# Layer 0's feed-forward network in two passes, context tokens first and then latent tokens by seven block products, with layer 1's last modulation moved into mixer 1

## The chip, the cores and the metric

The kernel runs on one core of one Trainium2 chip. The metric is the device time of one execution in microseconds. A run of this kernel is repeated, and the median stands; a profiled execution has a span (first to last instruction of the trace) and a device time of its own, a little longer than the span.

In the profile PE is TensorE (matrix products), PEld its loading of stationary operands, DVE is VectorE, ACT ScalarE, POOL GpSimd, and SP the engine that issues nearly all transfers. Engines run their instructions in order, each from a queue that is fixed when the kernel is built.

## The reference, cut to what matters

Two layers work on 512 latent tokens and 256 context tokens of width 1024. Each has a mixer (attention with input and output projections) and a SwiGLU feed-forward network (FFN) with 2816 hidden units. Every part is preceded by an RMS norm with shift and scale, and followed by a gate, all three from a modulation: a product of silu(c) with a matrix of 1024 x 6144 per layer.

```python
for l in range(DEPTH):
    last = l == DEPTH - 1
    mx = (s_c @ mod_w[l] + mod_b[l])[:, None, :]
    mc = (s_cc @ mod_w[l] + mod_b[l])[:, None, :]
    shx1, scx1, gx1, shx2, scx2, gx2 = jnp.split(mx, 6, axis=-1)
    ...
    x = x + gx1 * ax
    x = x + gx2 * _swiglu(_rms(x, norm_ffn_w[l]) * (1.0 + scx2) + shx2, ffn_w_in[l], ffn_w_out[l])
    if not last:
        ctx = ctx + gc1 * ac
        ctx = ctx + gc2 * _swiglu(_rms(ctx, norm_ffn_w[l]) * (1.0 + scc2) + shc2, ffn_w_in[l], ffn_w_out[l])

def _swiglu(h, w_in, w_out):
    gate, up = jnp.split(h @ w_in, 2, axis=-1)
    return (jax.nn.silu(gate) * up) @ w_out
```

After layer 0 both streams go on; layer 1's FFN is for the latent tokens only. Parts 0 to 5 of a modulation are shift, scale and gate of the mixer, then shift, scale and gate of the FFN.

## The kernel before: how the work is staged

All fp32 products are made of three products of fp32r pieces: an operand is split into a rounded high part and the rest, and high x high, high x low and low x high are summed in PSUM. So every weight that comes in by a transfer is cast on ACT (the high part) and subtracted on DVE or POOL (the low part) before TensorE may use it.

The stages in order are: start and modulation of layer 0; mixer 0 in four head groups; out-projection; layer 0's FFN; mixer 1 with eight heads, whose projections run a head ahead of the attention; out-projection; layer 1's FFN. Tile schedules the instructions by their order in the program and by its own estimate of times; where the program pins an engine's instructions, their order in that engine's queue is the program's.

Layer 0's FFN (`ffn`, called near the end of the layer 0 part) goes over hidden units in 11 pairs of 128. For each 128 it makes the gate and the up product for 512 latent and 256 context tokens together (L814: matmuls of 512 and of 256 columns, each with its own load of weights), then the hidden units, and for each pair the down products into `dps` (L869 to L871), which are gated and added to the residual by DVE (L439, L440). The modulation of layer 1 (24 chunks of 256 columns, `mod_chunks_by_pool`) is spread over these pairs by `MODS1`: ACT scales the rows (L213), POOL adds them up (L214 to L219), and TensorE then sums over partitions and turns the result (`modrow` L224, `modcol` L232) for up to four sums at a time. Context and latent tokens meet at the end in `done0`, the norm for layer 1.

Layer 1's FFN (`ffn_by_blocks`) treats 512 latent tokens and 128 hidden units at a time. Hidden blocks 0 to 3 are plain products; from block 4 on the gate and up products are made of seven products of half-size blocks in place of eight, each of 12 matmuls of 256 columns. That needs sums of weight blocks on POOL (`combine`, the tiles `ws`), sums of activation blocks once (`terms`, the tiles `tf`), and sums of the products on DVE (`after`). All instructions of this function are pinned.

Two rooms matter below. `raw_tile` has two slots for the whole kernel; out-projection weights, the rows of `ffn_w_out` (`wdr`), and the weights of mixer 1's projections (`wir`, L327, cast at L334, subtracted by POOL at L321) all land in it, and a slot is free again when the last reader is done. The pool `wr` of `ffn_by_blocks` has four slots, two hidden blocks' worth of gate and up weights.

Of the kernel before, what the change touches and what calls it, by code (L numbers as in the profile page):

```python
# [10 lines left out]
F32 = mybir.dt.float32  # L11
# [26 lines left out]
MODS1 = (2, 2, 2, 2, 2, 3, 3, 4, 4, 0)  # L38
# [25 lines left out]
def backbone(es: ExitStack, tc: tile.TileContext, x, c, ctx, c_ctx, mod_w, mod_b, norm_mix_w, norm_ffn_w,  # L64
# [11 lines left out]
    sc_pool = tc.tile_pool(name="p_sc", bufs=2, space=PSUM, reuse_waits="tile")  # L76
# [91 lines left out]
    def mod_chunk(l, part, n, new_tile, pool, bank, wide=None, room=("modr", 1)):  # L168
# [3 lines left out]
        ps = p_1.tile([P, width], F32, name="mod", tag=bank) if wide is None else \  # L172
            wide.tile([P, 1024], F32, name="mod", tag="sc")[:, :width]
# [7 lines left out]

        for i, k in enumerate([*range(kp, KT), *range(kp)]):
# [14 lines left out]
    def mod_chunks_by_pool(chunks, pool):  # L197
# [3 lines left out]
        for l, part, n, streams in chunks:  # L201
            c0 = part * D + n * width
            accs = [pool.tile([P, width], F32, name="ma", tag="ma", bufs=4) for _ in range(streams)]
            for pc in range(2):
# [3 lines left out]
                for i, acc in reversed(list(enumerate(accs))):  # L208

                    pr = pool.tile([P, 4, width], F32, name="modp", tag="mp", bufs=1) if i else w  # L210
                    for k in range(4):
                        kk = 8 * i + 4 * pc + k
                        nc.scalar.activation(pr[:, k], w[:, k], AF.Copy, scale=cols[:, kk:kk + 1])  # L213
# [6 lines left out]
            all_accs.extend(accs)  # L220
        ps = tr_tile("modrow", [P, width])
# [7 lines left out]
        nc.scalar.copy(r[:32 * m], ps[:32 * m])  # L229
        ps = tr_tile("modcol", [P, 2, m])  # L230
# [480 lines left out]
    def out_units(wp, w_out, subs=(nc.gpsimd.tensor_sub,), rooms=(raw_tile,)):  # L711
        for k in range(KT):
            def views(raw, k=k):
                yield raw, w_out[0, k * P:(k + 1) * P, :]
            yield unit(wp[k // 4], views, [P, D], 4, "wo", subs[k % len(subs)], rooms[k % len(rooms)])

    class OutProj:
# [31 lines left out]
        def some(self, ps, t, n, ks, first, last):  # L749
            ohi, olo = tile_T(0, t), tile_T(1, t)  # L750
            for k in ks:
                a, b = (z[:, n * 512:(n + 1) * 512] for z in self.ws[k])
# [22 lines left out]
        def last_sums(self, t):  # L775
            ohi, olo = tile_T(0, t), tile_T(1, t)
            ps = p_sc.tile([P, 1024], F32, name="ops", tag="sc")
            for k in range(KT):
                for x, j, q in ((ohi, 0, 0), (ohi, 1, 1), (olo, 0, 2)):
                    for n in range(2):  # L780
                        c = slice(n * 512, (n + 1) * 512)
                        nc.tensor.matmul(ps[:, c], x[:, k, :], self.ws[k][j][:, c],
# [4 lines left out]
    def ffn(l, xs, ntok, wp, fp, done, mods=()):  # L787

        n_tok = ntok * P
        segs = [(0, SEQ)] + ([(SEQ, TOK)] if ntok > NTX else [])  # L790
        first_segs = segs if ntok > NTX else [(0, SEQ // 2), (SEQ // 2, SEQ)]
        g = None
        wo, hid = [], []
        for p in range(NF // 2):
            def w_in(c0, name):
                res = []
                for u in range(2):
                    def views(raw, u=u):
                        yield raw, ffn_w_in[l, u * 512:(u + 1) * 512, c0:c0 + 256].rearrange(
                            "(j p) n -> p j n", p=P)  # L800
                    res.append(unit(wp[0].pool, views, [P, 4, 256], 4, name))
                return res
            wg, wu = w_in(p * 256, "wg"), w_in(FFN + p * 256, "wu")
            for j in range(2):
                def views(raw, j=j):
                    yield raw, ffn_w_out[l, (2 * p + j) * P:(2 * p + j + 1) * P, :]
                wo.append(unit(wp[1].pool, views, [P, D], 4, "wd"))
            def half(j, w, ps, sgs):
                for sg in sgs:
                    for k in range(KT):  # L810
                        whi, wlo = (z[:, k % 4, j * P:(j + 1) * P] for z in w[k // 4])
                        for a, b, q in ((whi, 0, 0), (whi, 1, 1), (wlo, 0, 2)):
                            for s0, s1 in sg:
                                nc.tensor.matmul(ps[:, s0:s1], a, cols_T(b, s0, s1)[:, k, :],  # L814
                                                 start=k == 0 and q == 0, stop=k == KT - 1 and q == 2)

            def places():
                if ntok > NTX:
                    return [p_sc.tile([P, 1024], F32, name=name, tag="sc")[:, :n_tok] for name in ("pg", "pu")]
                both = p_sc.tile([P, 1024], F32, name="pgu", tag="sc")  # L820
                return both[:, :SEQ], both[:, SEQ:]

            ps = []
            if p == 0 and ntok == NTX:
                ps = [places() for j in range(2)]
                for s in first_segs:
                    for j in range(2):
                        for w, z in zip((wg, wu), ps[j]):
                            half(j, w, z, [[s]])
            for j in range(2):  # L830
                if not (p == 0 and ntok == NTX):
                    ps.append(places())
                    if p == 0 and j == 0:
                        for s in first_segs:
                            for w, z in zip((wg, wu), ps[j]):
                                half(j, w, z, [[s]])
                    else:
                        for w, z in zip((wg, wu), ps[j]):
                            half(j, w, z, [segs])
                pg, pu = ps[j]  # L840
                sg = fp.tile([P, n_tok], F32, name="sg", tag="sg", bufs=1)
                nc.scalar.activation(sg, pg, AF.Silu)  # L842

                nc.vector.tensor_mul(pu, sg, pu)
                hid.append(split(fp, pu, [P, n_tok], "hd", 4))
            for i, mod in enumerate(mods[0] if p == 0 and mods else ()):
                mod_chunk(*mod, lambda shape, name: fp.tile(shape, F32, name=name, tag="mw", bufs=2), fp, f"tr{i % 2}", room=("ma", 4))
            if p and mods and mods[p]:
                mod_chunks_by_pool(mods[p], fp)
            if g is None:  # L850
                g = [gate_row(l, 5, i, fp) for i in range(2 if ntok > NTX else 1)]
            if p == NF // 2 - 2:

                continue
            nj = len(hid)
            whole = nj > 2 and ntok > NTX
            for t in CTX_FIRST[:ntok] if ntok > NTX else range(ntok):
                for n in range(2):
                    if whole and t == CTX_FIRST[0]:
                        ps = tr_tile("dps", [P, 512])  # L860
                    elif whole:
                        ps = acc_tile("dps")
                    else:
                        turn["sum"] = (turn["sum"] + 1) % 4
# [818 lines left out]
```

## Time and profile before

| what | us |
|---|---|
| device time, median of 3 runs (range) | 1773.58 (1773.14 to 1774.15) |
| device time of the profiled execution | 1773.26 |
| its span | 1771.4 |
| TensorE busy in the span | 1696.1 |
| VectorE busy | 1066.9 |
| ScalarE busy | 852.4 |
| GpSimd busy | 822.4 |
| layer 0's FFN, first to last product, roughly | 428 to 1002 |
| mixer 1 | 1002 to 1410 |
| layer 1's FFN | 1414 to 1771 |

A line of the profile's groups reads: line, engine, operation, written tile <- read tiles, shapes, count | busy us, mean ns of one | idle time just before it on that engine, and who ended it. A row of the timeline reads: start, duration, engine, line, operation, tiles, shapes, count, and in brackets the idle time before it and its releaser. A row of the windows view reads: the stretch, its length, busy us (and count) of PE, PEld, DVE, ACT and POOL, the granted TensorE clock, the busy share of the 16 DMA engines and GB/s.

### The profile page before, as it was taken

The page shows a single profiled execution, that of the slowest core. Times are in us where ns is not written, and L with a number is a line of the kernel's source. Part 1 is how long each engine was busy: PE and PEld are TensorE (multiplying, and loading weights), DVE is VectorE, ACT ScalarE, POOL GpSimd, SP SyncE. Part 2 cuts the span into 40 slices and gives each one's busy share as a digit, 9 for nine tenths or more (in the row PEclk, how much of TensorE's full clock was granted, in tenths as well). Part 3 has the DMA queues.
Part 4 walks back from the last instruction along what each step waited for, and adds up shares of the span by engine and source line. Part 5 has one row for each costly group of instructions (what it writes and reads, how often), then busy time and mean ns, then how long its engine had stood idle before and what let it go on. Part 6 is the DMA issues. An engine that isn't in the chain of part 4 may idle for free. (4 is left out here: it accounts for less than half of the span.)

```text
span 1771.4 us, 28187 instructions
## 1 busy us (share of the span) xinstructions
PE 1696.1 (96%) x10606; PEld 1471.0 (83%) x10606; DVE 1066.9 (60%) x1891; ACT 852.4 (48%) x1841; POOL 822.4 (46%) x1087
## 2 busy tenths in 40 slices
PE   6999999989999999999999999999988999999998
PEld 3887777767888888888888889999986798999997
DVE  4776555444365565554552665666664478877777
ACT  6556565443354444433332466666664345444441
POOL 2753333422054443312230657767772247777770
PEclk8999999999999999999999999999998999999999
DMA  9212233303443334433332211111122325333332
GB/s 319 55 43 73 84 96 108 107 25 119 143 144 97 105 108 155 131 110 108 105 119 62 94 37 36 37 36 51 43 84 83 96 72 161 92 95 107 107 96 95
DMA packets 176168, 169.96 MB, mean 96 GB/s; under 512 B 16608, under 2 KB 162592, under 8 KB 176032
## 3 DMA queue, kind: packets, MB, share of 16 engines
q1 hardware_dynamic: 175680, 167.96, 30.8%
q8 instruction: 83, 1.36, 0.3%
q14 instruction: 53, 0.43, 0.1%
q10 hardware_dynamic: 352, 0.21, 0.0%
HBM read 161.82 MB, written 6.32 MB: 95 GB/s over the span
## 5 line engine op out<-in xcount | busy, mean ns | idle before, releaser
L432 PE MATMUL inps<-wih,hT 128*128 128x384 f32 x384 | 132.9, 346 | 2.1 <-ACT qkv L630 2.0
L439 DVE TENSOR_TENSOR dps<-dps,g 128x512 f32<-128x512 f32 x128 | 87.8, 696 | 72.0 <-PE dps L871 57.6
L434 PE MATMUL inps<-wih,hT 128*128 128x384 f32 x384 | 130.8, 341 | 0.0
L433 PE MATMUL inps<-wil,hT 128*128 128x384 f32 x384 | 130.7, 340 | 0.0
L814 PE MATMUL pg<-hT,wgh 128*128 128x512 f32 x352 | 129.8, 392 | 0.0
L814 PE MATMUL pu<-hT,wuh 128*128 128x512 f32 x352 | 129.4, 391 | 0.4 <-DVE x L440 0.4
L213 ACT ACTIVATE modw<-modw,cols 128x256 f32<-128x256 f32 x192 | 82.0, 498 | 84.1 <-DMA modw<-in_mod_w_dram 80.4
L869 PE MATMUL dps<-wdh,hdh 128*128 128x512 f32 x264 | 106.3, 404 | 1.6 <-DVE x L440 1.6
L870 PE MATMUL dps<-wdl,hdh 128*128 128x512 f32 x264 | 104.5, 396 | 0.0
L871 PE MATMUL dps<-wdh,hdl 128*128 128x512 f32 x264 | 101.8, 396 | 0.0
L214 POOL TENSOR_TENSOR modw<-modw 128x512 f32<-128x512 f32 x48 | 62.1, 1294 | 84.5 <-ACT modw L213 84.5
L814 PE MATMUL pg<-hTc,wgh 128*128 128x256 f32 x352 | 98.1, 282 | 2.7 <-ACT hTc L308 2.4
L814 PE MATMUL pu<-hTc,wuh 128*128 128x256 f32 x352 | 97.8, 282 | 0.0
L321 POOL TENSOR_TENSOR wil<-wir,wih 128x256 fp32r<-128x256 f32 x84 | 68.2, 839 | 62.7 <-ACT wih L334 50.0
L886 PE MATMUL pg<-hT,wbh 128*128 128x256 f32 (+1 forms) x464 | 88.6, 288 | 1.6 <-DVE pg L886 1.6
L886 POOL TENSOR_TENSOR wbl<-ws,wbh 128x256 fp32r<-128x256 f32 x72 | 58.8, 847 | 64.2 <-PE pu L886 54.3
L440 DVE TENSOR_TENSOR x<-x,dps 128x512 f32<-128x512 f32 x128 | 85.2, 682 | 2.3
L552 ACT ACTIVATE Pt<-sc,nm 128x256 f32<-128x256 f32 (+3 forms) x96 | 68.0, 712 | 38.1 <-DVE nm L548 14.7
L886 POOL TENSOR_TENSOR ws<-wr 128x256 f32<-128x256 f32 x72 | 77.1, 1092 | 12.6 <-DMA wr<-in_ffn_w_in_dram 12.6
L886 PEld LDWEIGHTS pg<-hT,wbh 128*128 128x128 f32 x464 | 74.0, 188 | 6.2 <-DVE pg L886 1.8
L814 PEld LDWEIGHTS pg<-hT,wgh 128*128 128x128 f32 x352 | 66.0, 188 | 14.9 <-ACT sg L842 0.4
L814 PEld LDWEIGHTS pu<-hT,wuh 128*128 128x128 f32 x352 | 66.0, 188 | 14.9 <-issue 0.8
(332 smaller groups left out, 5507.1 us busy)
## 6 DMA issues: line engine op xcount, KB each, us to landing
modw<-in_mod_w_dram SPq DMA_DIRECT2D x96, 512.0 KB, 4.4
wdr<-in_ffn_w_out_dram SPq DMA_DIRECT2D x44, 512.0 KB, 3.7
wr<-in_ffn_w_in_dram SPq DMA_DIRECT2D x44, 512.0 KB, 5.2
wir<-in_od_w_in_dram SPq DMA_DIRECT2D x96, 128.0 KB, 2.3
wgr<-in_ffn_w_in_dram SPq DMA_DIRECT2D x22, 512.0 KB, 4.3
wur<-in_ffn_w_in_dram SPq DMA_DIRECT2D x22, 512.0 KB, 3.5
x<-in_x_dram SPq DMA_DIRECT2D x8, 512.0 KB, 6.8
wir<-in_ev_w_in_dram SPq DMA_DIRECT2D x16, 256.0 KB, 2.7
```

The lines of the kernel that those rows point to most:

```text
L213: nc.scalar.activation(pr[:, k], w[:, k], AF.Copy, scale=cols[:, kk:kk + 1])
L321: nc.gpsimd.tensor_sub(lo[c], raw[c], hi[c])
L432: nc.tensor.matmul(ps, hs[0][:, k, :], a, start=k == 0, stop=False)
L433: nc.tensor.matmul(ps, hs[0][:, k, :], b, start=False, stop=False)
L434: nc.tensor.matmul(ps, hs[1][:, k, :], a, start=False, stop=k == KT - 1)
L439: nc.vector.tensor_mul(tmp, ps, g[:, n * 512:(n + 1) * 512])
L440: eng.tensor_add(xt[:, n * 512:(n + 1) * 512], xt[:, n * 512:(n + 1) * 512], tmp)
L814: nc.tensor.matmul(ps[:, s0:s1], a, cols_T(b, s0, s1)[:, k, :], start=k == 0 and q == 0, stop=k == KT - 1 and q == 2)
L869: nc.tensor.matmul(ps, hh, a, start=j == 0, stop=False)
L870: nc.tensor.matmul(ps, hh, b, start=False, stop=False)
L871: nc.tensor.matmul(ps, hl, a, start=False, stop=j == nj - 1)
L886: return tc.keep_in_program_order(op(*args, **kw))
```

## The change

Layer 0's FFN is now made by `ffn_by_blocks` too, and `ffn` is gone.

1. A context pass: for all 22 hidden blocks the gate, up and down products of the 256 context tokens, plain, with the sums kept in `cacc`. Then a latent pass over all 22 blocks for the 512 latent tokens: blocks 0 and 1 plain, 2 to 21 by seven block products. Layer 0's FFN weights are loaded and split twice.
2. Between the passes POOL gates the context sums and adds the residual; they are parked in DRAM and come back for layer 1's norm near the end of the latent pass (`CtxPart.end`, `back`).
3. In mixer 0's last head group context tokens come before latent token tile 3 (`LAST_ORDER`); tiles 2 and 3 are normed inside the context pass.
4. Modulation: TensorE's steps are issued some blocks after the loads, behind TensorE's last instruction so far. Layer 0's last part (4 chunks, `mod_steps`) uses two `raw` slots in blocks 3, 7, 11 and 15, with its products one block later. Layer 1's parts 0 to 2 (12 chunks) are spread over the context pass, the second stream's scaling on POOL. Parts 3 to 5 (12 chunks) are summed by DVE in mixer 1, in `raw` slots, one chunk at a time.
5. In both layers' FFN end, two of four residual tiles are resumed by POOL and one by DVE earlier, and the last sums use other PSUM banks. Pinned instructions are chained by `issue_after`.

```diff
-MODS1 = (2, 2, 2, 2, 2, 3, 3, 4, 4, 0)
+MODS1 = (1, 1, 1, 1, 1, 1, 1, 1, 2, 2, 0)
+LAST_ORDER = (0, 1, 2, 4, 5, 3)
...
+    def mods_by_vector(chunk, pool):
...
+        def load(pc):
+            w = raw_tile([P, 4, width], "modw")
...
+        w = load(0)
+        yield
+        with behind(nc.vector):
+            add(w, 0)
+        w = load(1)
+        yield
+        with behind(nc.vector):
+            add(w, 1)
+        yield
+        with behind(nc.tensor):
+            for _ in mod_rows([chunk], [acc]):
+                pass
...
+            for f in range(NF):
+                nxt = Plain((f + 1) % NF)
+                d = down(f, cwd)
+                next(d)
+                two = [ctx_group(*tn, f < 4) for tn in four[f % 2 * 2:f % 2 * 2 + 2]] if f > 1 else []
+                ps = [p[:, :width] for p in places()]
+                for i in range(2):
+                    product(ps[0], cur.w[i], ct[i], i == 0, i == 1)
+                nxt.hi()
+                if last:
+                    next(last)
+                nxt.lo()
+                if last:
+                    end(last)
+                for g in two[:1]:
+                    next(g)
+                nxt.hi()
+                nxt.lo()
+                for i in range(2):
+                    product(ps[1], cur.w[2 + i], ct[i], i == 0, i == 1)
+                for g in two[:1]:
+                    end(g)
+                next(d)
+                nxt.hi()
+                nxt.lo()
+                for g in two[1:]:
+                    next(g)
+                last = hidden(ps, nc.scalar, dve, None, chid)
+                next(last)
+                next(d)
+                nxt.hi()
+                nxt.lo()
+                end(d)
+                for g in two[1:]:
+                    end(g)
+                if f % 2 and f > 1:
+                    del chid[:2], cwd[:2]
+                ctx_part.middle(f, fp)
+                cur = nxt
...
+            tt.terms()
+            for i in range(2):
+                product(ps[1], cur.w[2 + i], rows[i], i == 0, i == 1)
+            for _ in range(2):
+                nxt.hi(act)
+                nxt.lo()
+            for g in two[2:]:
+                next(g)
+            for g in two:
+                end(g)
+            for t in range(2):
+                pool.tensor_mul(cacc[t], cacc[t], g1)
+                pool.tensor_add(cacc[t], cacc[t], xs[NTX + t])
+            fp = ctx_part.end(cacc)
...
+            w = Weights(2)
...
+            for i in range(2):
+                product(ps[0], cur.w[i], rows[i], i == 0, i == 1)
+            w.sums1()
+            w.sums2()
+            w.sums3()
+            tt.split()
...
+            if f % 4 == 3 and self.rows:
+                steps = mod_steps(*self.rows.pop(0), raw_tile, pool, "tr0", room=("ma", 4))
+                next(steps)
+                self.late.append((f + 1, steps))
...
+            step = h * NTX + t
+            for m in moving:
+                next(m, None)
+            if step % 2 == 0 and step < 24:
+                moving.append(mods_by_vector((1, 3 + step // 8, step // 2 % 4, 1), at.pool))
+                next(moving[-1])
             emit((h + 1) * NT + 2 + (2, 3, 5, 6)[t])
```

`down` fetches `wdr` into a `raw` slot at its first step, casts it on ACT at its second and subtracts it on DVE, pinned, in two halves after that.

More of the change, by code (lines that the diff above doesn't have):

```diff
@@ L785, in last_sums @@
                 residual(self.xs[t], ps[:, n * 512:(n + 1) * 512], self.g[0 if t < NTX else 1], n)
[L787 to L864, printed above, removed]
-                        ps = p_1.tile([P, 512], F32, name="dps", tag=("acc0", "tr0", "acc1", "tr1")[turn["sum"]])
-                    for j in range(nj):
-                        hh, hl = (z[:, t * P:(t + 1) * P] for z in hid[j])
-                        a, b = (z[:, n * 512:(n + 1) * 512] for z in wo[j])
-                        nc.tensor.matmul(ps, hh, a, start=j == 0, stop=False)
-                        nc.tensor.matmul(ps, hh, b, start=False, stop=False)
-                        nc.tensor.matmul(ps, hl, a, start=False, stop=j == nj - 1)
-                    residual(xs[t], ps, g[0 if t < NTX else 1], n)
-                    if p == NF // 2 - 1:
-                        done(t, n)
-            wo, hid = [], []
@@ L877, in backbone @@
+    chain = {}
     class Pinned:
@@ L1203, in ffn_by_blocks @@
         hid, wd = [], []
[L1204 to L1213 removed]
+        pending = [(t, n) for t in range(NTX) for n in range(2)]
         def plain(ws):
```

471 lines of the change are left out of this document (346 added, 125 removed).

## The prediction

> **What bounds the kernel now.** I read the page's header and engine table first.
>
> ```profile
> span 1771.4 us, 28187 instructions
> PE 1696.1 (96%) x10606; PEld 1471.0 (83%) x10606; DVE 1066.9 (60%) x1891; ACT 852.4 (48%) x1841; POOL 822.4 (46%) x1087
> ```
>
> TensorE is busy in all but 75.3 us of the span. So the kernel gains where TensorE gets less to do, provided that the others keep up; an average over the span cannot say that, so the second view is the table of windows.
>
> ```profile
> 428.18:998.00 569.82, 565.23 (x3076) 477.43 (x3075) 296.77 (x411) 225.79 (x408) 184.83 (x189) 1.00 0.37 116
> 1060.00:1300.00 240.00, 231.89 (x1604) 221.85 (x1603) 150.72 (x298) 152.11 (x390) 171.89 (x299) 0.99 0.16 47
> 1450.00:1478.50 28.50, 28.50 (x136) 23.48 (x135) 26.11 (x24) 16.90 (x27) 16.94 (x14) 1.00 0.43 131
> 1478.50:1724.30 245.80, 245.80 (x1728) 228.72 (x1727) 191.39 (x320) 101.44 (x177) 188.12 (x199) 1.00 0.35 101
> ```
>
> Columns: the stretch, its length, busy us of PE, PEld, DVE, ACT and POOL, the granted clock, DMA share, GB/s. The first row is layer 0's FFN: 4.6 us idle in 569.8, so TensorE sets its time. The second is the middle of mixer 1, with 8.1 us idle in 240. The last two are layer 1's FFN: the step from plain products to block products, and 16 blocks with block products. TensorE never stops there, with VectorE at 78% and GpSimd at 77%: what layer 0 is to become exists already in layer 1, and there TensorE bounds it.
>
> The third view is the timeline of TensorE, for the price of a product.
>
> ```profile
> 1449.91 0.63 PE L886 MATMUL pu<-hT,wbh 128*128 128x512 f32 x2
> 1450.38 0.40 PE L886 MATMUL pu<-hT,wbl 128*128 128x512 f32 x1
> 1450.61 0.39 PE L886 MATMUL pu<-hT,wbh 128*128 128x512 f32 x1
> ```
> ```profile
> 448.08 0.40 PE L814 MATMUL pg<-hTc,wgh 128*128 128x256 f32 x2
> 448.31 0.28 PE L814 MATMUL pg<-hTc,wgl 128*128 128x256 f32 x1
> 448.43 0.28 PE L814 MATMUL pg<-hTc,wgh 128*128 128x256 f32 x1
> ```
>
> From start to start three of 512 columns take 0.70 us (0.2333 each), three of 256 take 0.35 (0.1167 each), each with its own weights. So 256 columns cost half of 512: a context pass by itself pays no more per column.
>
> **The change, part by part.** All against the profiled execution's own 1773.26 us (span 1771.4 and 1.86 around it); the median of the runs shown is 0.3 above it.
>
> *Block products: -28.0.* A hidden block's gate and up products are 48 of 512 and 48 of 256 columns, 16.8 us. After: 48 x 0.1167 = 5.6 in the context pass and 7 x 12 = 84 x 0.1167 = 9.8 in the latent pass, 15.4. That is 1.4 less in each of 20 blocks; blocks 0 and 1 and all down products cost what they did. The size is checked by the last window: 16 blocks in 245.8 us are 15.36 each, against 9.8 + 24 x 0.2333 (down) = 15.4.
>
> *Start: -3.0.* At the FFN's start TensorE waits for the context tokens' norm.
>
> ```profile
> 435.18 0.70 PE L814 MATMUL pu<-hT,wuh 128*128 128x512 f32 x2 [0.37 <-DVE x L440]
> 444.32 0.39 PE L814 MATMUL pg<-hTc,wgh 128*128 128x256 f32 x1 [2.44 <-ACT hTc L308]
> 445.05 0.39 PE L814 MATMUL pg<-hTc,wgh 128*128 128x256 f32 x1 [0.22 <-DVE hTc L309]
> ```
>
> `LAST_ORDER` norms context tokens before tile 3's attention ends, and tiles 2 and 3 have the whole context pass. The three waits, 0.37 + 2.44 + 0.22, go. If that cover fails the 3.0 stay.
>
> *Layer 1's end: -2.6.* The last down groups wait for banks that VectorE still reads.
>
> ```profile
> 1735.57 0.51 PE L886 MATMUL pg<-hT,wbh 128*128 128x256 f32 x2 [1.57 <-DVE pg L886]
> 1741.06 0.47 PE L886 MATMUL pu<-hT,wbh 128*128 128x256 f32 x2 [1.01 <-DVE quvw L886]
> ```
>
> Other banks and two residual tiles on GpSimd relieve VectorE just there: 1.57 + 1.01. Between 0 and -2.6.
>
> *Layer 0's end: +1.6.* It takes the same form, and mixer 1 follows at once. Between 0 and the 2.6 of the two rows above; I take the larger.
>
> *Slots in the context pass: +9.4 (0 to 32).* TensorE's block is now 48 x 0.1167 + 12 x 0.2333 = 8.4 us, in the order 2.8 (first product), 1.4 (down), 2.8, 1.4. Transfers and splits are as many as in a block of 25.2 before.
>
> ```profile
> modw<-in_mod_w_dram SPq DMA_DIRECT2D x96, 512.0 KB, 4.4
> wdr<-in_ffn_w_out_dram SPq DMA_DIRECT2D x44, 512.0 KB, 3.7
> ```
> ```profile
> L886 DVE TENSOR_TENSOR wbl<-wr,wbh 128x512 fp32r<-128x512 f32 x62 | 51.7, 839 | 6.5 <-ACT wbh L886 6.4
> L886 DVE TENSOR_TENSOR wdl<-wdr,wdh 128x512 fp32r<-128x512 f32 x44 | 38.4, 885 | 0.3 <-ACT wdh L886 0.3
> L886 DVE TENSOR_TENSOR x<-x,dps 128x512 f32<-128x512 f32 x64 | 43.6, 681 | 23.4 <-PE dps L886 23.4
> L886 ACT CAST wdh<-wdr 128x1024 fp32r<-128x1024 f32 x22 | 23.2, 1058 | 1.4 <-DMA wdr<-in_ffn_w_out_dram 1.3
> L886 ACT CAST wbh<-ws 128x512 fp32r<-128x512 f32 x72 | 41.8, 628 | 43.5 <-PE pg L886 31.9 <-POOL ws L886 11.6
> ```
>
> VectorE has 4 x 0.839 + 2 x 0.885 + 2 x 0.681 = 6.5 us a block, and a little for the hidden units: it keeps up. But in blocks 3, 7, 11 and 15 a chunk of layer 0's part 5 takes both `raw` slots, and its products stand behind block f+1's last TensorE instruction. `wdr` of block f+1 waits in SP's queue until then. Its cast stands in ACT's pinned queue ahead of the third weight piece of block f+2, and its subtraction in VectorE's ahead of the fourth. From the slot's release that is 3.7 + 1.06 + 0.63 + 0.84 + 0.885 + 0.84 = 7.96 us until the fourth piece is there; TensorE needs it after 2.8 + 1.4 + 1.4 = 5.6. So 2.36 us, four times, 9.4. It is 0 if the slots come free earlier than I read, and 4 x 7.96 = 32 if nothing covers it. Layer 1's 12 chunks here have slots of their own and as many groups of TensorE's steps (ten) as before.
>
> *From plain to block products in the latent pass: +6.5 (0 to 14.8).* GpSimd's pinned queue has four operations on the context sums (two gates, two adds, 1024 columns) ahead of the first sums of weight blocks, and these need VectorE's context adds first.
>
> ```profile
> L886 POOL TENSOR_TENSOR ws<-wr 128x256 f32<-128x256 f32 x72 | 77.1, 1092 | 12.6 <-DMA wr<-in_ffn_w_in_dram 12.6
> L886 POOL TENSOR_TENSOR ws<-ws,wr 128x256 f32<-128x256 f32 x36 | 42.5, 1200 | 0.0
> ```
> ```profile
> L886 DVE TENSOR_TENSOR tf<-tf,hT x4: 1642/1644/1649, 1448.8 to 1457.2; 128x1024 f32<-128x1024 f32 x4
> ```
> ```profile
> 1432.43 2.40 POOL L886 TENSOR_TENSOR tf<-hT 128x1024 f32<-128x1024 f32 x1 [13.31 <-DVE wbl L886]
> ```
>
> From the pass's start VectorE has four weight pieces (3.4), four down pieces (3.5), seven `tf` (11.5) and four context adds (2.7): 21.1 us. Then GpSimd: 4 x 2.40, 2 x 1.09, 2 x 1.20, and ACT's cast 0.63, which ends at 35.9. TensorE comes to the second block product after two plain blocks (22.4), the last context groups (5.6) and one block product (1.4), at 29.4. It waits 6.5. It is 0 where the sums are done beside the gating, as the row of 1450 to 1478.5 shows for layer 1, and 35.9 - 21.1 = 14.8 if TensorE had nothing left. I take the working, since the queue is written down.
>
> After such a wait the clock may matter.
>
> ```profile
> 20.00:30.00 10.00, 7.63 (x32) 6.27 (x32) 3.61 (x7) 6.41 (x12) 3.44 (x7) 0.50 1.08 366
> ```
>
> This stretch near the start, after long idling, had a granted clock of 0.50, while the FFN's row has 1.00 in spite of the 2.44 us wait. The Trainium skill, page "TensorE: Matmul & The Clock Gate", section "What's actually happening", says that about 3.4 us without work halve the clock until some 3.4 us of work have passed. By that rule, which speaks against the change, the 6.5 us would bring about 1.7 us more (an estimate from that page) and 1767.3 in all; the two rows agree with it, neither has a wait of this length.
>
> *Mixer 1: +8.4 (4.4 to 52).* Twelve chunks come as twelve groups of `modrow` and `modcol`.
>
> ```profile
> 530.85 0.40 PE L871 MATMUL dps<-wdh,hdl 128*128 128x512 f32 x1
> 531.18 0.64 PE L224 MATMUL modrow<-ma,cst 128*32 128x256 f32 x8
> 531.75 0.50 PE L869 MATMUL dps<-wdh,hdh 128*128 128x512 f32 x1
> ```
> ```profile
> 536.04 0.51 PE L232 MATMUL modcol<-cst,ma 128*128 128x4 f32 x4
> 536.41 0.48 PE L869 MATMUL dps<-wdh,hdh 128*128 128x512 f32 x1
> ```
>
> A group costs (531.75 - 530.85 - 0.23) + (536.41 - 536.04) = 0.67 + 0.37 = 1.04, twelve 12.5. Mixer 1's row has 8.1 us idle to take some of it; all of it would leave 4.4. I take half, 8.4. The rows of these chunks hold one of the two `raw` slots, and these feed the projections:
>
> ```profile
> 1191.57 0.83 ACT L334 CAST wih<-wir 128x768 fp32r<-128x768 f32 x1
> ```
> ```profile
> 1202.92 2.27 POOL L321 TENSOR_TENSOR wil<-wir,wih 128x256 fp32r<-128x256 f32 x3
> ```
> ```profile
> 1232.71 5.12 POOL L321 TENSOR_TENSOR wil<-wir,wih 128x256 fp32r<-128x256 f32 x6
> ```
> ```profile
> 1195.74 2.31 DMA wir<-in_od_w_in_dram
> ```
>
> With two slots a head's four weights take 1191.57 (the first one's cast) to 1205.19 (the last one's subtraction), 13.6 us. One after the other in a single slot they take 4 x (2.31 + 0.83 + 2.27) = 21.6, 8.0 more. The next head's subtractions start at 1232.71, so there is room and I take nothing for it; 6 heads x 8.0 = 48 beside the 4.4 is the upper end.
>
> *Sum:* -28.0 - 3.0 - 2.6 + 1.6 + 9.4 + 6.5 + 8.4 = -7.7; 1773.26 - 7.7 = **1765.6**.
>
> **The rivals.**
>
> *The waits are hidden.* Transfers start earlier than their place in the program, and GpSimd's late work falls into spare time: the two FFN waits at 0, mixer 1 at 4.4. 1773.3 - 33.6 + 1.6 + 4.4 = 1745.7. For it speaks the unbroken TensorE of layer 1; against it the slots, which are a written order.
>
> *Nothing in sum.* Mixer 1 at 12.5 and some more in the context pass: between 1769.7 and 1776.8.
>
> *Slower: mixer 1's weights through one slot.* The last chain of the profile goes through just these rows (transfer, cast, subtraction, transfer), so a slot that is held shows. If half of the 48 gets through, 24 more: 1789.6. It decides from (7.7 + 3.5) / 6 = 1.9 us a head. Against it: 27 us between the subtractions of one head and the next.
>
> *The context pass bound by transfers.* In 22 x 8.4 = 185 us there are 22 x 3 x 0.524 MB of weights, 16 chunks x 2 x 0.524 of modulation and 2.1 of residual: 53.5 MB, 289 GB/s. The start's row above moved 366 at full share, but in layer 1's start
>
> ```profile
> 1410.00:1425.00 15.00, 12.84 (x87) 12.01 (x86) 12.81 (x24) 11.26 (x24) 2.82 (x3) 0.89 0.93 259
> ```
>
> 259 was already a share of 0.93. At 259 the pass takes 207 us, 21.8 more in place of 9.4: 1778.0.
>
> That seven products don't save what they should is excluded by the last window.
>
> **How the numbers follow.** About 0.2% (3.5 us) is what a measurement of this kernel can tell from no change. Forecast 0.40, its own range 1755 to 1769.7; waits hidden 0.10; nothing in sum 0.12; mixer 1's slot 0.25; transfers 0.13. Faster is the first two, 0.50; same 0.12; slower 0.38. The range goes from 1750, which keeps half of the hidden case, to 1793, which takes in the transfers and most of the slot's case.
>
> **What would show it.** Blocks of 15.4 us in the latent pass without idle TensorE; no wait at the FFN's start; four waits of some 2.4 us for weights in the context pass after blocks 4, 8, 12 and 16; one of 6.5 at the second block product, released by a cast of `ws` after GpSimd; mixer 1 longer by about 8 with its weights' groups no longer than 22 us. Wrong would be: a context pass well over 195 us with the DMA share near 1, mixer 1 longer by 20 or more with TensorE waiting for projections, or seven-product blocks that wait on VectorE or GpSimd.

## The result, and the profile after

| | before | after |
|---|---|---|
| device time, median of 4 runs (range), us | 1773.36 (1769.9 to 1774.15) | 1969.26 (1961.81 to 1974.68) |
| span of the profiled execution, us | 1771.4 | 1965.2 |

The changed kernel is slower by a factor of 1.110 (95% interval 1.108 to 1.112). The page of the changed kernel begins:

```profile
span 1965.2 us, 30974 instructions
PE 1767.8 (90%) x11378; PEld 1534.8 (78%) x11378; DVE 1246.5 (63%) x2280; ACT 926.4 (47%) x1992; POOL 1075.6 (55%) x1350
```

TensorE is now idle for 197 us where it was 75, and its busy time has grown by 72, though the block products should take 28 us of products away. To see where, I cut both traces at the same events: first product of layer 0's FFN, (after only) first product of the latent pass, first projection of mixer 1, first product of layer 1's FFN, end. The windows of the kernel before, columns as in the prediction (36 of layer 0's down products, 8.4 us, stand behind the first projection there, and so in the second row):

```profile
428.18:997.97 569.79, 565.20 (x3075) 477.40 (x3074) 296.75 (x411) 225.79 (x408) 184.80 (x189) 1.00 0.37 116
997.97:1414.50 416.53, 392.44 (x2528) 361.18 (x2526) 251.80 (x497) 244.47 (x616) 249.13 (x423) 0.98 0.19 57
1414.50:1771.40 356.90, 348.81 (x2337) 319.26 (x2337) 280.24 (x431) 145.42 (x251) 221.10 (x222) 0.99 0.36 105
```

And of the changed kernel:

```profile
433.60:688.50 254.90, 217.42 (x1462) 188.20 (x1462) 154.22 (x243) 141.12 (x286) 159.91 (x173) 0.93 0.68 207
688.50:1069.94 381.44, 360.26 (x2361) 327.68 (x2359) 294.40 (x460) 154.82 (x267) 270.93 (x278) 0.97 0.38 111
1069.94:1608.20 538.26, 450.03 (x2557) 387.03 (x2555) 280.27 (x597) 249.47 (x621) 245.27 (x418) 0.90 0.21 64
1608.20:1965.20 357.00, 347.36 (x2337) 317.61 (x2337) 280.89 (x427) 145.28 (x251) 233.36 (x226) 1.00 0.35 105
```

The 193.8 us of span divide into +5.4 (start), +66.5 (layer 0's FFN: 254.9 + 381.4 for 569.8), +121.7 (mixer 1) and +0.1 (layer 1's FFN). In mixer 1 TensorE is idle for 88 us instead of 24, and the granted clock is 0.90 instead of 0.98. Its busy time has grown by 58 us. The twelve groups are 12.5 of them by the prediction's price, and 8.4 us of down products went out of this stage, so most of the rest are products at the lower clock.

What TensorE waits for most in that window and, below it, the wait for the other half of the same weights, from the changed kernel's waits (engine, who <- for whom: us, times, longest):

```profile
PE inps L495 <- POOL wil L383: 26.5, 19, 2.6
PE inps L494 <- ACT wih L396: 7.4, 11, 1.8
```

These two rows, the split of projection weights, were 1.4 us together before and are 34 of the 88 idle us now; the rest is spread over smaller waits inside the attention. SP's own waits say why the weights are late, before:

```profile
SPq L327 <- ACT wih L334: 150.5, 8, 26.4
SPq L327 <- POOL wil L321: 39.5, 18, 3.9
```

and after (L250 are the chunks' transfers, L389 the weights'):

```profile
SPq L250 <- DVE ma L258: 163.4, 10, 18.9
SPq L389 <- DVE ma L258: 45.2, 11, 8.2
SPq L389 <- POOL wil L383: 28.9, 14, 2.9
```

Before, SP stood 150 us with a transfer of the next head's weights in hand, waiting for ScalarE to take those that already lay in the slots: it ran ahead. One case is the gap that the prediction looked at: the second of the two slots was filled from 1205.21 us on, and ScalarE cast the first of them at 1231.31. After, SP stands for VectorE to add up a row (163 us), and weights stand behind rows. Its timeline around two heads:

```profile
1109.58 30.66 SPq L250 DMA_DIRECT2D modw<-in_mod_w_dram  x2
1148.19 17.13 SPq L389 DMA_DIRECT2D wir<-in_od_w_in_dram  x12
1168.23 36.53 SPq L250 DMA_DIRECT2D modw<-in_mod_w_dram  x4
1213.02 14.76 SPq L389 DMA_DIRECT2D wir<-in_od_w_in_dram  x12
```

From 1110 to 1140 SP issues two rows and nothing else: the row of 1109.58 is summed by VectorE only from 1137.6 on and holds its slot until then. From 1168 to 1205 it issues four rows. The weights between, from 1148 to 1165, come as TensorE already wants them, and it waits at that head's first products:

```profile
1163.96 0.38 PE L495 MATMUL inps<-wil,hTc 128*128 128x256 f32 x1 [2.59 <-POOL wil L383]
1166.09 0.58 PE L494 MATMUL inps<-wih,hTc 128*128 128x256 f32 x1 [0.51 <-ACT wih L396]
1168.26 0.58 PE L495 MATMUL inps<-wil,hTc 128*128 128x256 f32 x1 [1.59 <-POOL wil L383]
```

The windows around these rows:

```profile
1160.00:1165.00 5.00, 2.41 (x18) 2.12 (x18) 3.32 (x7) 1.76 (x4) 3.06 (x3) 1.00 0.27 79
1165.00:1170.00 5.00, 2.81 (x10) 1.73 (x8) 0.96 (x1) 1.66 (x2) 3.89 (x6) 0.53 0.37 102
1170.00:1175.00 5.00, 4.21 (x18) 3.92 (x19) 0.58 (x2) 0.98 (x3) 2.19 (x6) 0.50 0.58 186
```

The first product behind a wait of 2.59 us takes 0.38 us at a granted clock of 1.00; behind the next waits the same product of 256 columns takes 0.58, at 0.53. In a row without waits these products start 0.12 us apart in the first stretch and 0.21 apart in the last. The Trainium skill, page "TensorE: Matmul & The Clock Gate", section "What's actually happening", has the clock halved after an idle window of about 3.4 us. The halving agrees with the 0.50 here; but no wait of these rows is as long, the longest is 2.59 us, and the clock fell behind several close together. So a lack of work, not only one long stop, is paid twice: as idle time, and in slower products after it.

### The profile page after: what moved, and what is told of

It is laid out like the page before. It is cut to its first block, busy times and chain, and to the rows that moved or that the text cites. A ratio compares the mean times of both kernels' runs of the same rounds, so it can differ in the third digit from the quotient of the medians.

```text
span 1965.2 us, 30974 instructions
## 1 busy us (share of the span) xinstructions
PE 1767.8 (90%) x11378; PEld 1534.8 (78%) x11378; DVE 1246.5 (63%) x2280; ACT 926.4 (47%) x1992; POOL 1075.6 (55%) x1350
## 5 line engine op out<-in xcount | busy, mean ns | idle before, releaser
L875 PE MATMUL pg<-hT,wbh 128*128 128x256 f32 (+1 forms) x976 | 187.1, 289 | 11.5 <-DVE v L875 4.8
L875 DVE TENSOR_TENSOR wbl<-wr,wbh 128x512 fp32r<-128x512 f32 x218 | 185.1, 854 | 14.5 <-ACT wbh L875 9.5
L875 PEld LDWEIGHTS pg<-hT,wbh 128*128 128x128 f32 x976 | 156.2, 189 | 21.8 <-DVE v L875 5.2
L875 POOL TENSOR_TENSOR ws<-wr 128x256 f32<-128x256 f32 x152 | 156.8, 1052 | 15.2 <-DMA wr<-in_ffn_w_in_dram 15.2
L875 ACT CAST wbh<-ws 128x512 fp32r<-128x512 f32 x152 | 91.5, 626 | 129.3 <-PE pg L875 67.8
L875 PE MATMUL pg<-hT,wbl 128*128 128x256 f32 (+1 forms) x488 | 140.8, 288 | 2.9 <-DVE wbl L875 2.9
L875 DVE TENSOR_TENSOR wdl<-wdr,wdh 128x512 fp32r<-128x512 f32 x132 | 123.0, 938 | 32.0 <-ACT wdh L875 32.0
L875 PEld LDWEIGHTS dps<-wdh,hdh 128*128 128x128 f32 x408 | 78.3, 192 | 40.2 <-ACT hdh L929 16.5
L875 ACT CAST wbh<-wr 128x512 fp32r<-128x512 f32 x126 | 77.3, 619 | 61.2 <-issue 31.3
L495 PE MATMUL inps<-wil,hTc 128*128 128x256 f32 (+1 forms) x192 | 71.9, 375 | 28.3 <-POOL wil L383 26.5
L875 PEld LDWEIGHTS pg<-hT,wbl 128*128 128x128 f32 x488 | 92.3, 189 | 4.5 <-DVE wbl L875 3.1
L875 POOL TENSOR_TENSOR ws<-ws,wr 128x256 f32<-128x256 f32 x76 | 89.9, 1202 | 0.0
```

The source lines that it names most:

```text
L495: nc.tensor.matmul(ps, hs[0][:, k, :], b, start=False, stop=False)
L875: ins = op(*args, **kw)
```

## The experiments

Theory: the chunks' rows hold one of the two raw slots, and weights come late. Rivals: the work of the chunks itself (VectorE's sums, TensorE's groups in fixed places), or the place in SP's queue. Times below are spans of one profiled execution unless a ratio stands with them; stages go from first product to first product as above (the first expectation counts mixer 1 from 1046.0 us, 24 us earlier). Mixer 1 takes 538.3 us in the changed kernel and 416.5 before. Stages with the same or nearly the same instructions differ between runs: mixer 1 without chunks takes 403.7 to 410.7 us in eight runs, the context pass as changed 249.0 to 254.9 in nine, the latent pass 379.4 to 384.3 in sixteen. Most variants were executed once, so differences below some 7 us are not told apart.

**Mixer 1 without chunks (m_none).**

```
-            for m in moving:
-                next(m, None)
...
             if step % 2 == 0 and step < 24:
+                part, n = 3 + step // 8, step // 2 % 4
+                add_mod(1, part, 2 * n, 2 * n + 2, modc[1][:, part - 3, 2 * n:2 * n + 2, 0:1], 1)
```

> The changed kernel without the twelve chunks in mixer 1: no transfers, no VectorE sums, no TensorE groups; the values of parts 3 to 5 of layer 1's modulation are filled from parts 0 to 2 by a small VectorE operation, so this part of the computation is left out. The changed kernel's mixer 1 takes 562 us (1046.0 to 1608.2) where the kernel before takes 416.5. Theory (the chunks' rows hold one of two raw slots and stand ahead of the weights in SP's queue): mixer 1 falls to 416 to 425 and the whole to about 1823. Rival (VectorE sums and TensorE groups in their in-order queues): the same. Rival (something that the new feed-forward network leaves late at its end): mixer 1 stays above 500.

Measured: 1836.85 us (median of 2), 1.036 of before (1.032 to 1.039); mixer 1 409.1, below the 416 to 425 that both theories gave. The chunks cost 129 us of mixer 1, and nothing is left late by the stages before it. The other 61 us of span over the kernel before are +5.7 at the start and +62.5 in layer 0's FFN (249.1 + 383.2 for 569.8), less 7.4 in mixer 1, where the 8.4 us of down products no longer stand.

**Only the transfers and slots (m_loads).** `add` becomes a copy of one column, and the groups go.

```
-            add(w, 0)
+            nc.vector.tensor_copy(acc[:, 0:1], w[:, 0, 0:1])
```

> The chunks' transfers stay, in the same raw slots and the same queue, and each is released by one VectorE copy of one column at the same place; the 96 sums and 12 TensorE groups are left out, and parts 3 to 5 filled as without the chunks. Theory (slot and queue): mixer 1 stays above 530 us, at least 110 of the 146 remain. Rival (the work): below 445.

**Only the work (m_work).** `load` goes; the sums read the normed tokens.

```
-        w = load(0)
+        w = f32(hT[0][0])[:, 0:4, 0:width]
-        w = load(1)
```

> The 96 VectorE sums and 12 TensorE groups stay at their places, but read a tile that is resident (the normed tokens) in place of the rows; the 24 transfers and their use of the raw slots are left out, so parts 3 to 5 are wrong numbers. Theory (slot and queue): mixer 1 at 420 to 440 us (12.5 of groups and little else). Rival (the work): above 520.

Measured: mixer 1 459.2 with the transfers alone, 445.1 with the work alone: 50 and 36 us over 409.1. In both runs neither theory's range held: slot and work each cost something alone. The two make 86 of the 129. The other 43 come only when both are there; the reading that a slot is then held by a row whose sum stands late in VectorE's queue is tested by m_woe below.

**Another queue (m_poolq).** `nc.gpsimd.dma_start` in place of `nc.sync.dma_start` for the rows.

> As the changed kernel, but the chunks' 24 transfers are issued by GpSimd's queue in place of SP's; the raw slots are used as before. If what costs is the place in SP's queue (weights behind a row that waits for its slot): mixer 1 below 460 us. If it is the slot itself: above 530. If GpSimd's own queue then stands behind the wait for a slot: also above 530, with GpSimd's subtractions of weights late behind its own issue.

Measured: mixer 1 543.6. SP's order isn't what decides: without the rows in its queue, SP's weights still wait 154.3 us for VectorE's sums and 146.6 for the rows' transfers, that is, for slots that rows hold. Whether GpSimd's queue added a wait of its own isn't told apart by this run.

**Other room (m_woe).** The rows land where the first out-projection weights will lie from head 6 on.

```
-            w = raw_tile([P, 4, width], "modw")
+            w = woe.pool.tile([P, 4, width], F32, name="modw", tag=("whi", "wlo")[pc], bufs=2)
```

> As the changed kernel, the whole computation; only the rows of mixer 1's chunks land in room that is free until head 6 (the slots of the first output projection weights) in place of the two raw slots. SP's queue, VectorE's sums and TensorE's groups as in the changed kernel. The sums and groups alone cost 38 us over none (1872.2 against 1832.4 of span), the slots and transfers alone 49, both together 133. Theory (the held raw slot is what the sums make long: the sum stands late in VectorE's queue, the slot stays held and the weights come later still): the interaction goes with the slot, 1865 to 1885 in all. Rival (SP's queue: the weights' transfers stand behind a row's transfer whatever room it waits for): above 1930.

Measured: span 1865.3, mixer 1 438.3, its granted clock 0.97. One line of room takes back 100 of the 129 us with SP's queue, sums and groups unchanged, as the theory had it (1865 to 1885 in all). Its waits in mixer 1:

```profile
PE inps L495 <- POOL wil L383: 4.1, 4, 1.9
```
```profile
SPq L389 <- ACT wih L396: 39.8, 6, 25.0
```

TensorE's wait for weights falls from 26.5 to 4.1, and SP again runs ahead of ScalarE, though less (39.8 us of waiting for it, 150.5 before). The held slot is shown as the main cause.

**Groups later (m_woe_late), products by TensorE (m_pe).** What is left over 409.1 is 29 us. The first adds a `yield` ahead of the groups; the second drops VectorE's sums, and TensorE multiplies the rows (`mod_steps`).

> The whole computation, with the rows of mixer 1's chunks in free room as in m_woe, and TensorE's groups one step (some 13 us) later than VectorE's second sum. In m_woe mixer 1 took 438 us, without chunks 409, with products by TensorE 421. If TensorE standing at a group for a sum that isn't there is what remains over the 12.5 of the groups: 420 to 428. If VectorE's sums in its order cost it: within 4 of 438.

> The whole computation; mixer 1's chunks with the same free room, and the rows multiplied by TensorE itself (eight products per chunk, as layer 0's part 5 is made) in place of VectorE's sums and the one-row group. A chunk costs TensorE about 1.1 + 0.45 us by the rows of the context pass (64 products 4.3 us, 8 transposes 1.8), 12 chunks 19. Theory (what is left with own room is the sums' place in VectorE's and TensorE's queues): 1840 to 1860, less than half of the 38 remain. Rival (any interruption of TensorE's order in mixer 1 costs the same): within 8 us of the run with own room and VectorE's sums.

Measured: mixer 1 429.4 and 421.4. A step's delay takes 9 of the 29: less than the 10 expected at least, more than the 4 of the rival. Without VectorE's sums 12.3 remain, below the 19 expected of their products; m_pe's whole, 1850.27 us, lies in its range. That m_pe takes away 17 is clear of the spread; how the 29 divide between groups that stand for a sum, VectorE's sums and TensorE's own time is not, at these sizes.

**The context pass.** It takes 254.9 us in the changed kernel and 249.1 in m_none, on which the next runs build. The changed kernel's waits of TensorE and VectorE there:

```profile
PE pg L875 <- DVE wbl L875: 10.7, 4, 4.6
PE dps L875 <- DVE modsum L208: 9.1, 4, 3.4
PE dps L875 <- ACT nhc L366: 5.6, 1, 5.6
PE dps L875 <- ACT hdh L929: 5.3, 3, 3.0
PE npt L361 <- ACT nhc L366: 3.7, 1, 3.7
PE pu L875 <- DVE x L502: 3.1, 1, 3.1
```
```profile
DVE wdl L875 <- ACT wdh L875: 30.7, 4, 8.8
```

Four waits of VectorE for the down weights, up to 8.8 us, and four of TensorE for a weight piece: the events that the prediction described, 2.7 us each on average where it had 2.36. But they are a small part of what the pass is too long.

Rows in the chunks' slots (n_rows): `pool.tile(..., tag="mw", bufs=2)` for `raw_tile` in `mod_steps`.

> As the changed kernel without the chunks in mixer 1, and with the rows of layer 0's part 5 in the two slots that layer 1's chunks use, so that they hold no raw slot. The context pass (first to last product of the context tokens) takes 249 us there. Theory (rows in raw slots stop the down weights and so VectorE's and ScalarE's pinned queues): the waits for a weight piece (10.7 us) and for VectorE's sum of the rows (9.1) go or shrink to a third, the pass takes 225 to 238. Rival (the chunks' work and transfers, or the transfers of the weights themselves, set the pass): within 6 us of 249.

Without layer 1's chunks (n_nochunks), and without any (n_neither): `add_mod` from other parts' values in their place.

> Without the chunks in mixer 1, and without layer 1's twelve chunks in the context pass (parts 0 to 2 filled from layer 0's values by small VectorE operations: left out); the rows of layer 0's part 5 stay in the raw slots. Theory (rows' slots): 215 to 240, the four waits for weight pieces stay. Rival (the chunks' 12.6 MB and their work on ScalarE and GpSimd): below 212, near the 185 to 190 of TensorE's own work.

> Without the chunks in mixer 1, in the context pass neither layer 1's chunks nor layer 0's part 5 (both filled, left out). What is left are weights, their splits and products. If splits and transfers of weights keep up with TensorE: 184.8 us of products and a few for the norms of tiles 2 and 3, 190 to 197. If transfers of weights bind (34.6 MB at the 206 GB/s of the changed kernel's pass are 168 us, but in bursts) or VectorE's 6.5 to 7.3 us in 8.4: above 210.

Measured: 249.4, 209.6 and 194.2 us. Rows in other slots gain nothing as long as layer 1's chunks are there: the waits for weight pieces go, others come (the rows' transfers 8.9, GpSimd's sums 9.5). So the rival's figures held in the first two runs, and n_neither's range held. The chunks cost 40, the rows 15, and splits and transfers of weights alone nearly keep up with TensorE (8.2 us idle in the pass). In n_nochunks TensorE waits for no weight piece, though the rows lie in the raw slots: what it waits for there with the rows is VectorE's `modsum`, 7.3 us in four waits.

Transfers alone (c_loads) and work alone (c_work), both without the rows. In the first each row is released by one column's copy, in the second the scaling and sums use two resident tiles.

```
-                steps = mod_chunks_by_pool(parts[:n], pool)
...
+                        nc.gpsimd.tensor_copy(acc[:, 0:1], w[:, 0, 0:1])
```

```
-                w = pool.tile([P, 4, width], F32, name="modw", tag="mw", bufs=2)
...
+                w = held[pc]
```

> No chunks in mixer 1 and no rows of layer 0's part 5 (filled); of layer 1's twelve chunks in the context pass only the 24 transfers stay, in their own two slots and at their places in SP's queue, each released by one GpSimd copy of one column; scaling, sums and TensorE's groups are left out. The pass takes 194.2 us without any chunk. If transfers (12.6 MB among 34.6 of weights, and the place in SP's queue) cost the 40 us: above 222. If the work does: below 204.

> As c_loads, but the other half: scaling on ScalarE and GpSimd, GpSimd's sums and TensorE's ten groups stay and work on two resident zeroed tiles; the 24 transfers are left out, so parts 0 to 2 are wrong numbers. If the work (ScalarE's and GpSimd's and TensorE's groups behind it) costs the 40 us: above 222; if the transfers: below 204. GpSimd's scaling and sums run beside the splits, so the same figure also shows in how long VectorE's pieces take (839 ns in the kernel before).

Measured: 199.4 and 229.3 us, 5 and 35 over 194.2. The work costs, the transfers don't. Rows of the groups by shape, 440 to 640 us, show one way how. With the transfers alone, where GpSimd is busy for 15 of the 200 us:

```profile
L875 DVE TENSOR_TENSOR wbl<-wr,wbh 128x512 fp32r<-128x512 f32 x90 | 63.5, 710 | 4.6 <-ACT wbh L1232 4.6
L875 DVE TENSOR_TENSOR cacc<-cacc,dps 128x512 f32<-128x512 f32 x36 | 24.8, 688 | 38.7 <-PE dps L875 38.7
```

and with the work alone, where it is busy for 161:

```profile
L875 DVE TENSOR_TENSOR wbl<-wr,wbh 128x512 fp32r<-128x512 f32 x78 | 72.4, 933 | 4.8 <-ACT wbh L1232 4.8
L875 DVE TENSOR_TENSOR cacc<-cacc,dps 128x512 f32<-128x512 f32 x30 | 20.4, 680 | 5.8 <-PE dps L875 5.8
```

The same subtraction takes VectorE 710 ns with GpSimd nearly idle and 933 beside it, while its sums with one operand in PSUM (`dps`) take 688 and 680. The Trainium skill, page "SBUF — State Buffer", section "SBUF: two separate sides", says that VectorE with two SBUF inputs and GpSimd share a port pair and that the later one stands. These rows agree: of the two operations only the one with two SBUF inputs got slower. The other way is ScalarE's order, in c_work:

```profile
ACT modw L230 <- POOL modp L228: 47.3, 24, 6.2
```

ScalarE scales in place and must not overwrite the rows before GpSimd has read them for the second stream; casts of weights stand behind. To tell the two apart, ScalarE got the second stream back (d_act).

```
-                        if i:
-                            nc.gpsimd.tensor_scalar(pr[:, k], w[:, k], cols[:, kk:kk + 1], 1.0, ALU.mult, ALU.mult)
-                        else:
-                            nc.scalar.activation(pr[:, k], w[:, k], AF.Copy, scale=cols[:, kk:kk + 1])
+                        nc.scalar.activation(pr[:, k], w[:, k], AF.Copy, scale=cols[:, kk:kk + 1])
```

> Without the chunks in mixer 1 (filled, left out); the second stream of the chunks in the context pass is scaled by ScalarE again, as in the kernel before, and not by GpSimd. With GpSimd the pass took 249.1 us, with 29.7 us of ScalarE waiting for GpSimd before it may overwrite the rows. If that wait in ScalarE's order is the cause: 225 to 240. If GpSimd beside VectorE is the cause (its sums, 12 x 3.3 + 8 x 3.3 us, stay, its 64 scalings of 0.70 go): a third at most goes, 240 to 249. ScalarE gets 64 x 0.5 = 32 us more, which would show as above 249 if ScalarE binds.

Measured: 265.7 us, 17 longer. The wait for GpSimd is gone, and ScalarE has 27.4 us more work in its place: its queue is on the path, and the move to GpSimd was a gain. How the 35 us divide between ScalarE's time and VectorE's slower pieces stays open; in c_work TensorE's longest waits are for ScalarE's hidden units (`hdh`, 10.1 us in five) and none is for a weight piece, which speaks for ScalarE's queue.

**The step to block products (n_nogate).** The four GpSimd operations on the context sums are left out. The changed kernel's TensorE there:

```profile
720.96 0.50 PE L875 MATMUL pg<-hT,wbh 128*128 128x256 f32 x2 [3.49 <-ACT wbh L875]
724.33 0.58 PE L875 MATMUL pg<-hT,wbl 128*128 128x256 f32 x1 [2.87 <-DVE wbl L875]
735.65 0.79 PE L875 MATMUL dps<-wdh,hdh 128*128 128x512 f32 x1 [5.95 <-ACT hdh L875]
```

> Without the chunks in mixer 1 and without GpSimd's four operations that gate the context sums and add the residual (left out, 4 x 2.40 us). Theory (these stand ahead of the first sums of weight blocks in GpSimd's pinned queue): the waits of 3.5 (cast of a weight sum) and 2.9 us (its low part) at the second block product go, and of the 5.9 us before the down products a part; 6 to 10 us in all. Rival (VectorE's chain of terms, splits and context adds sets it): less than 2 us.

Measured: the latent stage 375.9 us for 383.2 in m_none, 7.3 less, and 3.5 below the shortest of the sixteen others. The wait for the cast goes; 2.8 and 5.0 us of the other two stay, so the three waits shrink by 4.6 (12.4 in m_none). TensorE's idle time in the stage shrinks by 2 us only, as other waits grow, and its busy time by 5, with a granted clock of 0.98 for 0.96. What the last of them stands for shows in ScalarE's rows of the changed kernel:

```profile
731.07 0.62 ACT L875 CAST wbh<-ws 128x512 fp32r<-128x512 f32 x1 [3.82 <-POOL ws L875]
731.59 0.59 ACT L875 ACTIVATE sg<-pg 128x512 f32<-128x512 f32 x1
```

The hidden units' first step (`sg`) stands in ScalarE's queue behind a cast that waits for GpSimd's sum of weights.

**All chunks by TensorE (best1), with a bank of their own (best2).** m_pe, and in the context pass one chunk per block by `mod_steps` in the chunks' slots; then the down sums there on three banks.

```
+            if 1 <= f <= 16:
+                l, part, n = self.rows.pop(0) if f % 4 == 3 else parts.pop(0)[:3]
+                steps = mod_steps(l, part, n, lambda shape, name: pool.tile(shape, F32, name=name, tag="mw", bufs=2),
+                                  pool, "tr0", room=("ma", 4))
```

> The whole computation; as with TensorE's products in mixer 1, and in the context pass also all sixteen chunks by TensorE's products, one chunk per block from block 1 on, in the two slots of the changed kernel's chunks, none in raw slots, nothing by ScalarE or GpSimd. The context pass takes 254.9 us in the changed kernel, 209.5 without layer 1's chunks and 194.2 without any. If it was the work on ScalarE and GpSimd and the raw slots: 205 to 220, and 1800 to 1825 in all. If it was the transfers of the rows: above 240.

> The whole computation, as best1, but the down sums of the context pass use three PSUM banks and leave the fourth to the chunks' products. In best1 the down products waited 16.5 us, eight times, for ScalarE's copy out of the shared bank. If that bank costs what the waits say: the pass 224 to 232 and 1818 to 1832 in all. If something else takes their place (transfers, which are the same): above 238.

Measured: context pass 243.8, then 214.8 us. The first lies above the 240 that was to speak for the rows' transfers, the second below the 224 to 232 expected, with the same transfers: they were not the cause. In best1 a new wait took the place of the old ones:

```profile
PE dps L875 <- ACT modr L200: 16.5, 8, 2.9
```

With a free bank it goes, and 29 us go with it, more than this row says: 20.5 us of idle time, and 8.5 of busy time, as the granted clock goes from 0.93 to 0.98. Times are 1843.52 us (1.038 of before, 1.028 to 1.047) and 1812.37 us (1.022, 1.016 to 1.028). best2 computes everything and is 157 us faster than the changed kernel, but the kernel before was faster in every run. Even n_neither, which leaves all of layer 1's modulation and a part of layer 0's out, has 1780.78 us.

## Why the prediction was wrong, point by point

It forecast a gain of 7.7 us in a range of 1750 to 1793; the time is 1969.

- *Block products, -28.0: right in their price.* The first `t3h` products of blocks in the latent pass follow each other by 15.41 to 15.43 us until the last four, as worked out. But the gain doesn't arrive: without any chunk (n_neither) layer 0's FFN takes 577.3 us, and the kernel before 578.2 with the 8.4 us of down products behind the first projection, its chunks included. TensorE's idle time in the stage is 31.3 us there and 4.6 in the kernel before.
- *Mixer 1, +8.4: the step that failed.* "There is room and I take nothing for it" read the 27 us between two heads' subtractions as free. They were not: the slots stood full with the next head's weights (SP's 150 us of waiting for ScalarE). A row in a slot takes that lead, and stays until VectorE comes to its sum. 121.7 us came by the stages' bounds, 129 against the same stage without chunks, over the upper end of 52, because that end priced the weights one after the other at full readiness and neither the row's own stay nor the clock. The rival of the held slot was the right mechanism at a fifth of its price (24 us more).
- *Slots in the context pass, +9.4: seen, but not what the pass costs.* The four waits for a weight piece came, 10.7 us in all. But with the rows in other slots the pass is as long (n_rows), and without layer 1's chunks the waits don't come (n_nochunks). The 15 us between n_nochunks and n_neither hold the rows' own products and the waits for `modsum` too.
- *Layer 1's chunks in the context pass: priced at nothing, cost 40.* "Slots of their own and as many groups" counted TensorE's steps alone. Per us the chunks are about as dense as before (12 in 255 us, 24 in 570), but the weights of 22 blocks are now split in 255 us instead of 570. That a block of 25 us had room on ScalarE and VectorE for a chunk's work and one of 8.4 has not is the reading; c_work and d_act fit it, but no run shows it by itself. The rival of a pass bound by transfers was wrong in its cause: transfers alone cost 5, and the DMA share in the changed kernel's pass is 0.68, not near 1.
- *Step to block products, +6.5: 12.3 measured.* Without the gating the wait for the cast went, and 4.6 us of the three waits with it, so GpSimd's queue was read rightly. Missed was the wait for block 1's hidden units, whose first step stands behind another cast that waits for GpSimd, and the clock: from 715 to 740 us it was granted 0.77 and then 0.66.
- *Start, -3.0: failed.* The kernel before began with latent tokens' products at 428.18 us; now the first product comes at 433.60, after a wait of 3.06 for a residual sum, and two waits for the norm's ScalarE steps bring 5.6 and 3.7 inside the pass.
- *Layer 0's end, +1.6: too small.* Waits of 1.10, 2.71, 1.09 and 3.97 us stand there.
- *Layer 1's end, -2.6: none.* 2.58 us of waits became 4.45, in a stage of 357.0 us for 356.9:

```profile
1923.80 0.51 PE L875 MATMUL pg<-hT,wbh 128*128 128x256 f32 x2 [2.05 <-DVE v L875]
1927.07 0.50 PE L875 MATMUL pu<-hT,wbh 128*128 128x256 f32 x2 [0.20 <-DVE w L875]
1930.95 0.50 PE L875 MATMUL pg<-hT,wbh 128*128 128x256 f32 x2 [2.20 <-DVE pg L875]
```

- *The clock: taken out of the sum.* It was priced, if at all, at 1.7 us in one place. It weighs where waits are many: mixer 1 was granted 0.90 and the context pass 0.93. The points of this list don't add up to the whole, since each wait also slows the products behind it, and no run takes the clock apart by itself.

## What to carry to other kernels

A buffer that looks idle between two bursts may be full of the next burst: look at what its transfer queue waits for before lending it out. A holder's stay counts up to its last reader's turn in that engine's queue, not its transfer. Work that was hidden over a long stage must be priced again for every engine when the stage shrinks.

## What had not been expected of the hardware

A VectorE subtraction of 128x512 fp32 with both inputs in SBUF took 710 ns with GpSimd nearly idle and 933 ns beside it; a sum of the same size with one input in PSUM took 688 and 680. Waits of 0.5 to 2.6 us, close together, were enough for a granted clock of 0.50, with products of 256 columns every 0.21 us in place of 0.12.
